# A planner that orders TensorE's work: due steps joined behind a generator's products, and new charges on its clock

## The chip, the core and the metric

The kernel runs on one core of a Trainium2 chip. Its engines are TensorE (PE: matmuls out of SBUF into PSUM), VectorE (DVE), ScalarE (ACT), GpSimd (POOL) and SyncE (SP, which issues DMAs). Each takes its instructions in the order in which the program emits them. The metric is device time of one execution, in microseconds (us); the median of three runs is given for the kernel before.

## What is computed

Two layers of a hybrid backbone over 256 context tokens and 256 latent tokens, width 2048, in float32. Cut to what matters here:

```python
for l in range(2):
    shift, scale, gate = split(silu(c) @ ada_w[l] + ada_b[l])        # for context and latent
    xn = rmsnorm(h) * (1 + scale) + shift
    u  = xn @ w_in[l]                      # one wide projection: r, k, v, pool, gates, decay, iclr, merge
    r, k, v = token-shifted parts of u
    S = S * w_t + (S @ -kk_t) (kk_t a_t)^T + v_t k_t^T               # a scan over the tokens,
    y = S @ r_t                                                      # 16 heads of 64, two directions
    y_a = (groupnorm(y) + bonus) * silu(gate_a) @ w_out_a
    y_b = (pool_mixer(u) * silu(gate_b)) @ w_out_b
    h = h + gate * ((mg0 * y_a + mg1 * y_b) @ w_out)
out = rmsnorm(h_lat) * final_g
```

In the second layer the context part is only needed up to its final state, so most products have 256 columns there instead of 512.

## The kernel before, in words

**Main stream.** The large projections are cut into units (class `Main`). A unit of 128 output channels runs over chunks of weights; each weight tile is loaded by SP (`wr`), rounded to `whi` by ACT, and DVE takes the rest as `wlo`. A step is three fp32r matmuls into `ps_mm` (`xh,whi`, `xl,whi`, `xh,wlo`). Loads are issued up to LA = 6 chunks ahead of the step that is emitted. `ps_st` is the group that starts a layer; `ps_ada` are the modulation's float32 products (128 rows by 2 or 4 columns), zipped into other units; `ps_mix` is the pool mixer.

**Generators.** The recurrence is done in chunks of 64 tokens for pairs of heads (8 pairs, each in two halves of four chunks). Python generators emit it step by step. `prep` makes the decays and keys of a pair (`ps_kk`, `ps_d`, `ps_a` of 512 columns, `ps_b`); `inv` inverts the chunk's triangular matrix by levels, in float16 (`ps_M`, then `ps_Z` and `ps_W` in turns, `ps_R`, `ps_X`, `ps_T`, `ps_V`); `chain` carries the state over the chunks (`ps_z`, `ps_a`, `ps_p`, `ps_y`, float32 products of 64 columns); `gnorm` is the group norm (`ps_c`, `ps_v`). Layer 1 runs two `inv` generators side by side, layer 0 one. Each step waits in the data for ACT or DVE work on the result of the step before it, and a generator yields the time at which its next step is due. For a step with products that is mostly `mg + rdy(inputs)`: the time at which the planner thinks the inputs are ready, plus a margin `mg` of 1000 ns in layer 0 and 600 ns in layer 1. A pair `(time, n)` also asks that n of the three PSUM buffers of the pool `piv` are free.

**The emission clock.** The order of everything is fixed while the program is built. `E["pe"]`, `E["dve"]`, `E["act"]` are clocks of the planner. Each emitted instruction moves its engine's clock (`clk`): to the latest of the engine's clock, the release of the output's buffer and the readiness of the inputs, plus a charge. A result is ready a lag later (200 ns behind PE, 140 ns behind ACT and DVE). None of this is executed on the chip; it only decides who comes next in each engine's queue.

**The loop `run`.** It goes through the generators in an order of priority (chain, gnorm, inverses, prep, open_y). The first whose due time is not later than `E["pe"]` is taken. If none is due, the main stream emits a batch of NS = 2 steps (six matmuls) if its weights are ready before the earliest due time; then the loop looks again. If the main stream isn't ready, the clock jumps to the earliest due time.

**The tiling of a matmul.** A matmul uses as many rows and columns of the array as its operands have: `128*128` in the rows of the trace is 128 rows by 128 columns. `ps_mm`, `ps_Z`, `ps_T` and the products of prep and gnorm are 128*128, `ps_W`, `ps_a` (64 columns) and one kind of `ps_y` 64*64, `ps_z`, `ps_p`, `ps_V` and the other `ps_y` 128*64, `ps_M` 64*128, `ps_ada` 128*4 or 128*2.

Of the kernel before, what the change touches and what calls it, by code (L numbers as in the profile page):

```python
# [8 lines left out]
R32 = mybir.dt.float32r  # L9
# [21 lines left out]
NU = (0, 1)  # L31
ZD = (0, 0)
N1, LA0, G0, LAG = 2, 20, 2, 4
AH, PACE, MG = 400.0, 600.0, (1000.0, 600.0)

V_MU, V_W0, V_A0, V_KK, V_KA, V_RK = 0, 24, 40, 56, 64, 80
# [10 lines left out]
def kernel(  # L47
# [65 lines left out]
    E = dict(pe=0.0, act=0.0, dve=0.0, pool=0.0, sp=0.0)  # L113
    rt, rd, old = {}, {}, {}

    def nm(ap):
        return ap.tensor.name
# [4 lines left out]
    def clk(eng, cost, o, ins, lag=60.0):  # L122
        t = max(E[eng], rd.get(old.get(nm(o)), 0.0))
        for a in ins:
            t = max(t, rt.get(nm(a), 0.0))
        t += cost
        E[eng] = t
        rt[nm(o)] = t + lag
        for a in ins:
            rd[nm(a)] = t + lag  # L130
# [29 lines left out]
    def size(ap):  # L160
        n = 1
        for s in ap.shape[1:]:
            n *= s
        return n

    def mm(out, lhsT, rhs, start=True, stop=True, dep=True):
        nc.tensor.matmul(out=out, lhsT=lhsT, rhs=rhs, start=start, stop=stop)  # L167
        n, m = size(rhs), size(lhsT)
        dt = lhsT.dtype
        if dt == F32:  # L170
            c = 110 if m <= 32 else 360 if n < 32 else 1.6 * n if n > 64 else 190 if m > 64 else 78
        elif dt == R32:
            c = max(0.4225 * n, 109) + 75 * (kind[0] != dt)
        else:
            c = 28 if m > 64 else 18
        kind[0] = dt
        clk("pe", c, out, (lhsT, rhs) if dep else (), 200.0)

    kind = [R32]

    def act(out, in_, func=AF.Copy, scale=1.0, bias=None):
        kw = {} if bias is None else dict(bias=bias)
        nc.scalar.activation(out=out, in_=in_, func=func, scale=scale, **kw)  # L183
        c = (50 if psum(in_) else 90) + 0.84 * size(out) + 93 * ((not isinstance(scale, float)) + (bias is not None))
        clk("act", c, out, (in_,), 140.0)
# [50 lines left out]
    def do_late(force=False):  # L236
        i = 0
        while i < len(late):
            if force or late[i][0] <= E["pe"]:
                late.pop(i)[1]()  # L240
            else:
                i += 1
# [247 lines left out]
    def proj(src, nk, rhs, ts_, post, ck=4, **kw):  # L490
        st = {}
        n = ts_.stop - ts_.start

        def pre():
            st["ps"] = pmm.tile([128, T], F32, tag="mm", name="ps_mm")

        def mk(k):
            def step(c):
                ps = st["ps"][:, 0:n]
                rh, rl = rhs(k)  # L500
                q = k % ck
                mm(ps, c["h"][:, q, :], rh[:, ts_], start=(k == 0), stop=False)
                mm(ps, c["h"][:, q, :], rl[:, ts_], start=False, stop=False)
                mm(ps, c["l"][:, q, :], rh[:, ts_], start=False, stop=(k == nk - 1))
            return (k // ck, step)

        return Unit(pieces(src, 2 * ck, ck), [mk(k) for k in range(nk)], pre, lambda: post(st["ps"][:, 0:n]), **kw)
# [4 lines left out]
    def due(x):  # L512

        return max(x[0], piv.free("iv", x[1])) if isinstance(x, tuple) else x

    def run():

        while True:
            do_late()
            best, bt, held = None, None, True  # L520
            for g in gens:
                while g[1] is None:
                    g[1] = next(g[0], "end")
                    if g[1] is None:
                        break
                    held = False
                if g[1] == "end" or g[1] is None:
                    continue
                t = due(g[1])
                if best is None or t < bt:  # L530
                    best, bt = g, t
                if t <= E["pe"]:
                    best, bt = g, t
                    break
            gens[:] = [g for g in gens if g[1] != "end"]
            if best is None or bt > E["pe"]:
                mt = M.time()
                if mt is not None and (best is None or max(mt, E["pe"]) <= bt):
                    for _ in range(NS):
                        M.step()  # L540
                        do_late()
                        mt = M.time()
                        if mt is None or mt > E["pe"] + SL:
                            break
                    continue
            if best is None:
                if not gens and M.empty():
                    break
                if late:
                    do_late(True)  # L550
                elif held:
                    raise RuntimeError("stuck")
                continue
            E["pe"] = max(E["pe"], bt)
            best[1] = next(best[0], "end")
        do_late(True)

# [91 lines left out]
    def phase_a(l):  # L649
# [7 lines left out]
        rhs = lambda k: (xh[k], xl[k])  # L657
# [5 lines left out]
        def chk(hf, j, d):  # L663
            return hf * 4 + (j if d == 0 else 3 - j)
# [300 lines left out]
        def inv(hfs, n16, nlo, zb):  # L965
            for p in range(NP):
                for hf in hfs:
                    while not fl["prep"][p]:
                        yield None
                    idx = p * 2 + hf  # L970
                    while fl["mm"] < idx or idx >= 2 and not fl["chain"].get((p - 1, hf)):
                        yield None
                    fl["mm"] = idx + 1
                    yield from inv_half(p, hf, n16, nlo, zb, hf if len(hfs) == 1 else 0)

        def inv_half(p, hf, n16, nlo, zb, u):
# [10 lines left out]
            for q in range(2):  # L987
                pm = [piv.tile([128, 2, 2, 128], F32, tag="iv", name="ps_M") for _ in range(2)]
                for j2 in range(2):
                    for d in range(2):  # L990
                        c = chk(hf, 2 * q + j2, d)
# [38 lines left out]
            ps = piv.tile([128, 8, 64], F32, tag="iv", name="ps_Z")  # L1030
# [17 lines left out]
            for lev in range(1, 6):  # L1048
                yield mg + rdy(X), 1
                ps = piv.tile([128, 8, 64], F32, tag="iv", name="ps_Z")  # L1050
# [30 lines left out]
            ps = piv.tile([128, 4, 2, 64], F32, tag="iv", name="ps_R")  # L1081
# [10 lines left out]
            ps = piv.tile([128, 4, 2, 64], F32, tag="iv", name="ps_X")  # L1092
# [15 lines left out]
            for q in range(2):  # L1108
                ps = piv.tile([128, 2, 2, 128], F32, tag="iv", name="ps_T")
                for j2 in range(2):  # L1110
                    for d in range(2):
                        c = chk(hf, 2 * q + j2, d)
                        nc.tensor.transpose(ps[:, j2, d, :], BK[:, d, c % 4].rearrange("p a t -> p (a t)"), ident)  # L1113
                        clk("pe", 120, ps, (), 200.0)
                act(BKt[:, 2 * q:2 * q + 2], ps)
            if last:
                yield from wait()
# [1 line left out]
            ps = pch.tile([128, 4, 64], F32, tag="ch", name="ps_V")  # L1119
# [381 lines left out]
    with tc.manual_schedule():  # L1501
# [68 lines left out]

        M.q2 += ada_blocks(1, KD, 2, pre0=to_1)
        run()
        B1 = A[2]
        rs = B1["p"].tile([128, TC], F32, tag="rs", name="rs")
# [112 lines left out]
```

## Time and profile before

| what | us |
|---|---|
| median of 3 runs (3052.47 to 3059.95) | 3058.64 |
| the profiled execution, its own time | 3058.09 |
| its span, first to last instruction | 3056.3 |
| busy: PE, PE's weight loads | 2906.3, 2292.5 |
| busy: DVE, ACT, POOL | 1820.7, 1457.3, 149.7 |
| mean granted TensorE clock, as a share of the full one | 0.978 |

A row of the timeline has the start in us from the span's start, a duration, engine and line, and what is written from what. Ends of matmuls are modelled, so neighbouring matmuls overlap in it and a difference of starts is the better measure of what one costs. A row of waits sums the idle time of an engine by the instruction that ended it.

### The profile page before, as it was taken

Reading aid. Unit: us, or ns where it says so; the run is one execution under the profiler, and the core shown is the slowest. Engines: PE = TensorE matmul, PEld = TensorE weight load, DVE = VectorE, ACT = ScalarE, POOL = GpSimd, SP = SyncE. Lnnn points to the kernel's source line nnn. Section 1 sums busy time; section 2 is a strip of 40 time slices with the busy share of each in tenths; the row PEclk is TensorE's granted clock in tenths of the full one; section 3 lists DMA queues with packets and bytes.
Section 4 is the critical chain, followed back from the end, with each engine's and each line's share of the span. In section 5 each row is a group of like instructions: output and inputs, shape, how many; then the busy total and the mean of one; then the engine's idle time right before and its main releaser. Section 6 shows DMA issues by size and latency. Waiting matters only on the chain.

```text
span 3056.3 us, 66262 instructions
## 1 busy us (share of the span) xinstructions
PE 2906.3 (95%) x27122; PEld 2292.5 (75%) x27122; DVE 1820.7 (60%) x4171; ACT 1457.3 (48%) x3092; POOL 149.7 (5%) x211
## 2 busy tenths in 40 slices
PE   5999999999999999998999989999999989999897
PEld 2687777767777777776876657887887768888797
DVE  3475666565655655534443235886786667775575
ACT  3254445445554554533222223666556646666454
POOL 2200000000000000000000002000000000000000
PEclk8999999999999999998999999999999989999899
DMA  9732222232333222327657764432333343344875
GB/s 361 256 121 72 78 76 91 72 116 94 112 111 118 87 80 87 94 88 248 205 190 225 234 222 124 141 117 85 108 94 111 119 127 99 111 122 129 260 251 161
DMA packets 158482, 427.74 MB, mean 140 GB/s; under 512 B 17376, under 2 KB 53600, under 8 KB 154080
## 3 DMA queue, kind: packets, MB, share of 16 engines
q1 hardware_dynamic: 133120, 390.32, 40.5%
q10 hardware_dynamic: 25056, 33.17, 3.0%
q8 instruction: 213, 3.49, 0.5%
q14 instruction: 93, 0.76, 0.1%
HBM read 389.21 MB, written 34.21 MB: 139 GB/s over the span
## 4 chain that ended last, share of the span: by engine, by line
PE 78%; DVE 8%; DMA 7%; ACT 5%; issue 2%; SPq 0%; POOL 0%; DVEq 0%; ACTq 0%; POOLq 0%
PE ps_mm L167 54%; PE ps_st L167 4%; DMA wr<-in_w_o 3%; DVE wlo L191 3%; PE ps_W L167 3%; PE ps_M L167 2%; PE ps_ada L167 2%; PE ps_y L167 2%; PE ps_a L167 2%; DMA wr<-in_w_in 2%; PE ps_Z L167 1%; PE ps_z L167 1%; PE ps_p L167 1%; ACT whi L183 1%; PE ps_T L1113 1%
## 5 line engine op out<-in xcount | busy, mean ns | idle before, releaser
L167 PE MATMUL ps_mm<-xh,whi 128*128 128x512 f32 (+1 forms) x2448 | 914.8, 374 | 8.2 <-ACT whi L183 3.1
L191 DVE TENSOR_TENSOR wlo<-wr,whi 128x512 fp32r<-128x512 f32 (+1 forms) x932 | 636.7, 696 | 444.8 <-ACT whi L183 439.1
L183 ACT ACTIVATE whi<-wr 128x512 fp32r<-128x512 f32 (+1 forms) x932 | 567.1, 619 | 671.3 <-PE ps_mm L167 336.7
L167 PE MATMUL ps_mm<-xh,wlo 128*128 128x512 f32 (+1 forms) x2448 | 855.2, 349 | 16.4 <-DVE wlo L191 15.7
L167 PE MATMUL ps_mm<-xl,whi 128*128 128x512 f32 (+1 forms) x2448 | 851.1, 348 | 0.0
L167 PEld LDWEIGHTS ps_mm<-xh,whi 128*128 128x128 f32 x2448 | 465.6, 190 | 91.9 <-issue 7.9
L167 PEld LDWEIGHTS ps_mm<-xh,wlo 128*128 128x128 f32 x2448 | 465.8, 190 | 83.5 <-DVE wlo L191 22.5
L167 PEld LDWEIGHTS ps_mm<-xl,whi 128*128 128x128 f32 x2448 | 467.6, 191 | 46.3 <-issue 1.0
L167 PE MATMUL ps_mm<-mgh,whi 128*128 128x512 f32 (+1 forms) x512 | 181.2, 354 | 2.9 <-ACT whi L183 2.9
L1024 DVE CAST_PREDICATED X<-pm_t,ps_W 128x128 f16<-128x128 uint8 x640 | 141.7, 288 | 65.2 <-PE ps_W L167 63.8
L167 PE MATMUL ps_mm<-mgh,wlo 128*128 128x512 f32 (+1 forms) x512 | 175.4, 343 | 0.0
L167 PE MATMUL ps_mm<-mgl,whi 128*128 128x512 f32 (+1 forms) x512 | 174.5, 341 | 0.0
L167 PE MATMUL ps_mm<-yh,whi 128*128 128x512 f32 (+1 forms) x512 | 129.0, 344 | 0.2 <-ACT whi L183 0.2
L167 PEld LDWEIGHTS ps_mm<-mgh,whi 128*128 128x128 f32 x512 | 98.2, 192 | 38.9 <-issue 19.3
L167 PE MATMUL ps_mm<-yl,whi 128*128 128x512 f32 (+1 forms) x512 | 125.4, 337 | 0.6 <-DVE m L195 0.5
L183 ACT ACTIVATE VS<-P 64x128 f32<-64x128 f32 x128 | 39.3, 307 | 167.3 <-DVE P L195 164.8
L183 ACT ACTIVATE zb<-ps_Z 128x512 f16<-128x512 f32 x144 | 85.2, 592 | 70.2 <-PE ps_Z L167 68.8
L167 PEld LDWEIGHTS <-X 64*64 64x64 f16 x2560 | 89.4, 110 | 35.7 <-issue 27.5
L191 POOL TENSOR_TENSOR nlo<-MM,n 64x512 f16<-64x512 f32 x48 | 62.8, 1308 | 1072.2 <-DVE X L1024 760.2
L167 PEld LDWEIGHTS ps_mm<-mgh,wlo 128*128 128x128 f32 x512 | 98.3, 192 | 14.5 <-DVE wlo L191 3.6
L167 PEld LDWEIGHTS ps_mm<-mgl,whi 128*128 128x128 f32 x512 | 98.4, 192 | 8.7
L167 PE MATMUL ps_ada<-wr,svp 128*4 128x256 f32 (+1 forms) x1024 | 83.2, 402 | 22.8 <-DMA wr<-in_ada_w 22.8
(258 smaller groups left out, 4353.2 us busy)
## 6 DMA issues: line engine op xcount, KB each, us to landing
wr<-in_w_in SPq DMA_DIRECT2D x306, 512.0 KB, 3.7
wr<-in_ada_w SPq DMA_DIRECT2D x128, 512.0 KB, 3.9
wbig<-in_ada_w SPq DMA_DIRECT2D x32, 1024.0 KB, 6.0
wr<-in_w_o SPq DMA_DIRECT2D x64, 512.0 KB, 4.8
wr<-in_w_b SPq DMA_DIRECT2D x32, 512.0 KB, 4.8
wr<-in_w_a SPq DMA_DIRECT2D x32, 512.0 KB, 4.0
wr<-in_w_st SPq DMA_DIRECT2D x32, 384.0 KB, 4.3
d_mg<-mth ACTq DMA_DIRECT2D x32, 256.0 KB, 2.0
```

Source lines behind the costliest of these rows:

```text
L167: nc.tensor.matmul(out=out, lhsT=lhsT, rhs=rhs, start=start, stop=stop)
L183: nc.scalar.activation(out=out, in_=in_, func=func, scale=scale, **kw)
L191: ENG[eng].tensor_tensor(out=out, in0=a, in1=b, op=op)
L1024: nc.vector.copy_predicated(dst.rearrange(pat, **kw)[:, :, :, u, :], m, src.rearrange(pat, **kw)[:, :, :, u, :])
L1113: nc.tensor.transpose(ps[:, j2, d, :], BK[:, d, c % 4].rearrange("p a t -> p (a t)"), ident)
```

## The change

`mm` gets new charges. It keeps the tiling of the product before (`mode`, each side rounded up to 32, 64 or 128) beside its type, charges 104 ns when the tiling changes, and 80 ns when an fp32r product follows another type at the same tiling. float32 products are charged by columns and by their share of the array. A transpose is charged 220 ns instead of 120. `count` counts the products. In `run`, `was` is the count at the end of the last main batch. While products of a generator have been emitted since (`count[0] != was`), steps that are due up to JOIN = 600 ns later than the clock are taken as well, by generators' priority; the clock is not moved forward to their due time. Behind a main batch the limit is the clock itself, as before.

```diff
+JOIN = 600.0
@@ mm
-        n, m = size(rhs), size(lhsT)
+        n, m, r = size(rhs), size(lhsT), lhsT.shape[0]
         dt = lhsT.dtype
+        up = lambda x: 32 if x <= 32 else 64 if x <= 64 else 128
+        mode = (up(r), 128 if dt == R32 else up(m))
         if dt == F32:
-            c = 110 if m <= 32 else 360 if n < 32 else 1.6 * n if n > 64 else 190 if m > 64 else 78
+            c = max(1.667 * n, 60) * mode[0] * mode[1] / 128 ** 2 * (2 if mode == (64, 64) else 1) + 5
         elif dt == R32:
-            c = max(0.4225 * n, 109) + 75 * (kind[0] != dt)
+            c = max(0.417 * n, 60) + 13
         else:
-            c = 28 if m > 64 else 18
-        kind[0] = dt
+            c = 29 if m > 64 else 16
+        c += 104 if mode != kind[1] else 80 if dt == R32 != kind[0] else 0
+        kind[:] = dt, mode
+        count[0] += 1
         clk("pe", c, out, (lhsT, rhs) if dep else (), 200.0)
-    kind = [R32]
+    kind = [R32, (128, 128)]
+    count = [0]
@@ run
+        was = -1
         while True:
             do_late()
+            now = E["pe"] + (JOIN if count[0] != was else 0)
...
-                if t <= E["pe"]:
+                if t <= now:
...
-            if best is None or bt > E["pe"]:
+            if best is None or bt > now:
...
+                    was = count[0]
                     continue
...
-            E["pe"] = max(E["pe"], bt)
+            E["pe"] = max(E["pe"], bt - JOIN if bt <= now else bt)
@@ inv_half
-                        clk("pe", 120, ps, (), 200.0)
+                        clk("pe", 220, ps, (), 200.0)
```

## Rows read from the trace of the kernel before

**Rows 1.** The head of the page and its first part: the span; busy time, share of the span and instructions of an engine.

```profile
span 3056.3 us, 66262 instructions
...
PE 2906.3 (95%) x27122; PEld 2292.5 (75%) x27122; DVE 1820.7 (60%) x4171; ACT 1457.3 (48%) x3092; POOL 149.7 (5%) x211
```

**Rows 2.** The page's fourth part: shares of the chain of work that ended last.

```profile
PE 78%; DVE 8%; DMA 7%; ACT 5%; issue 2%; SPq 0%; POOL 0%; DVEq 0%; ACTq 0%; POOLq 0%
```

**Rows 3.** The table by stage, for the two stretches in which generators run: start and end, length, busy us (instructions) of PE, PEld, DVE, ACT and POOL, granted clock, DMA share, GB/s.

```profile
190.00:1394.00 1204.00, 1187.39 (x11215) 892.72 (x11217) 695.83 (x1625) 577.83 (x1233) 43.99 (x55) 1.00 0.31 95
...
1900.00:2850.00 950.00, 900.22 (x10973) 766.10 (x10972) 688.25 (x1736) 577.40 (x1305) 48.33 (x58) 0.97 0.39 117
```

**Rows 4.** PE's timeline: the first product of the first and of the last visit of generators, of 335 in layer 0 and of 310 in layer 1.

```profile
203.01 0.38 PE L167 MATMUL ps_M<-AR,BK 64*128 64x128 f32 x2
...
1380.18 0.40 PE L167 MATMUL ps_v<-gqh,bo_r 128*128 128x512 f32 x1
...
1930.10 0.40 PE L167 MATMUL ps_kk<-kqh,bo_r 128*128 128x512 f32 x1
...
2835.03 0.58 PE L167 MATMUL ps_v<-gqh,bo_r 128*128 128x256 f32 x1
```

**Rows 5.** PE's timeline in layer 0: a main matmul, a visit of ps_W (first and last of its 16 rows), the first two main matmuls behind it.

```profile
599.77 0.39 PE L167 MATMUL ps_mm<-xh,wlo 128*128 128x512 f32 x1
600.09 0.22 PE L167 MATMUL ps_W<-zb,X 64*64 64x64 f16 x2
...
600.59 0.20 PE L167 MATMUL ps_W<-X,zb 64*64 64x64 f16 x2
600.71 0.50 PE L167 MATMUL ps_mm<-xh,whi 128*128 128x512 f32 x1
601.04 0.39 PE L167 MATMUL ps_mm<-xl,whi 128*128 128x512 f32 x1
```

**Rows 6.** PE's timeline in layer 0: a visit of ps_Z, one batch of the main stream (first two and last of its six matmuls), a visit of ps_z.

```profile
280.23 0.39 PE L167 MATMUL ps_mm<-xl,whi 128*128 128x512 f32 x1
280.46 0.39 PE L167 MATMUL ps_mm<-xh,wlo 128*128 128x512 f32 x1
280.69 0.41 PE L167 MATMUL ps_Z<-X,n 128*128 128x64 f16 x8
280.93 0.47 PE L167 MATMUL ps_mm<-xh,whi 128*128 128x512 f32 x1
281.24 0.39 PE L167 MATMUL ps_mm<-xl,whi 128*128 128x512 f32 x1
...
282.17 0.40 PE L167 MATMUL ps_mm<-xh,wlo 128*128 128x512 f32 x1
282.49 0.45 PE L167 MATMUL ps_z<-VS,MM 128*64 128x64 f32 x8
```

**Rows 7.** The same in layer 1, where the main matmuls have 256 columns: ps_Z, one batch, ps_a.

```profile
2597.69 0.28 PE L167 MATMUL ps_mm<-xh,wlo 128*128 128x256 f32 x1
2597.81 0.41 PE L167 MATMUL ps_Z<-X,n16b 128*128 128x64 f16 x8
2598.05 0.36 PE L167 MATMUL ps_mm<-xh,whi 128*128 128x256 f32 x1
2598.26 0.28 PE L167 MATMUL ps_mm<-xl,whi 128*128 128x256 f32 x1
2598.37 0.28 PE L167 MATMUL ps_mm<-xh,wlo 128*128 128x256 f32 x1
...
2598.73 0.28 PE L167 MATMUL ps_mm<-xh,wlo 128*128 128x256 f32 x1
2598.94 0.45 PE L167 MATMUL ps_a<-Zs,X 64*64 64x64 f32 x8
```

**Rows 8.** ACT's timeline: what wrote VS ahead of the ps_z of rows 6, and Zs ahead of the ps_a of rows 7; in brackets the idle time before it and who ended it.

```profile
279.86 0.31 ACT L183 ACTIVATE VS<-P 64x128 f32<-64x128 f32 x1 [1.22 <-DVE P L195]
...
2597.20 0.26 ACT L183 ACTIVATE Zs<-ps_z 128x128 f32<-128x128 f32 x1
```

**Rows 9.** PE's waits in 190 to 1394 us: who waited for whom, us in total, times, longest.

```profile
PE ps_ada L167 <- DMA wr<-in_ada_w: 8.0, 5, 3.3
PE ps_ada L167 <- DVE ada_r L206: 4.5, 6, 2.1
...
PE ps_p L167 <- DVE VS L200: 1.2, 2, 0.9
```

**Rows 10.** PE's timeline in layer 1: a visit with two steps, ps_W (its last row) and ps_p, and the main matmul behind it.

```profile
2600.72 0.20 PE L167 MATMUL ps_W<-X,zbb 64*64 64x64 f16 x2
2601.10 0.78 PE L167 MATMUL ps_p<-VS,BKt 128*64 128x64 f32 x8 [0.18 <-ACT VS L183]
2601.80 0.38 PE L167 MATMUL ps_mm<-xh,whi 128*128 128x256 f32 x1
```

**Rows 11.** PE's waits in 1900 to 2850 us: the main stream's longest, and the first and last of the twelve rows in which a generator's product waits (ps_T, ps_a, ps_b, ps_W, ps_z, ps_M, ps_Z, ps_p; 12.5 us together).

```profile
PE ps_mm L167 <- DVE wlo L191: 14.4, 15, 2.2
...
PE ps_T L1113 <- DVE MM L191: 3.0, 1, 3.0
...
PE ps_p L167 <- ACT VS L183: 0.2, 1, 0.2
```

## The prediction

> **What bounds the kernel.** I read the page first. PE is busy for 2906.3 of 3056.3 us, DVE for 1820.7 [rows 1], and 78% of the chain of work that ended last is PE [rows 2]. So a microsecond of PE time is a microsecond of the kernel, unless somebody else becomes late. The table by stage comes next: the generators (recurrence, inverses, preparation, group norm) run in two stretches, 190 to 1394 us (layer 0) and 1900 to 2850 us (layer 1), 2154 us together [rows 3]. Outside them there is nothing to join. The reader should note DVE: 695.8 of 1204 us (58%) in the first stretch, 688.3 of 950 us (72%) in the second.
>
> The PE timeline comes last, since it shows what a generator's visit costs. Call every run of generator products between two pieces of the main stream a visit. I walked along all the rows of PE and count 335 visits in layer 0 and 310 in layer 1; the first and last of each are in [rows 4]. Behind 106 of the 335 and 150 of the 310, the main stream put out one batch only (two steps, six or seven matmuls) before the next visit. Those are what the change can join.
>
> **The price of a visit.** Starts of neighbouring matmuls tell it. Main matmuls of 512 columns follow each other after 0.23 us, of 256 columns after 0.12. Into a visit whose tiling is not 128x128 the step is 0.32 (599.77 to 600.09), so 0.09 more. Out of it the last product takes 0.12 (600.59 to 600.71), where its pair took about 0.03 inside the visit (16 pairs from 600.09 to 600.59), so 0.09 to 0.10 more. The first main matmul behind it takes 0.33 (600.71 to 601.04), 0.10 more [rows 5]. Together 0.29 us. A visit of ps_Z keeps 128x128: it enters at 0.23 (280.46 to 280.69), but the first main matmul behind it takes 0.31 (280.93 to 281.24), so 0.08 to 0.09 [rows 6]; the same in layer 1, 0.21 for 0.12 (2598.05 to 2598.26) [rows 7]. A joined pair therefore saves 0.29 where both have one tiling, 0.19 where the tilings differ (one change stays between them), and 0.09 where one of the two is 128x128.
>
> A rule can be set against this. The rows show 0.31 behind ps_Z, with no tiling changed [rows 6]. The Trainium skill (TensorEngine Tiling (Array Packing), Key Properties) prices another thing: "Changing tiling mode (not just tile) drains the TensorE"; by it alone a joined ps_Z would save nothing. What that makes of the sum is a rival below; the sum itself goes by the rows.
>
> **Part 1, JOIN.** Behind products the planner also takes a step that is due within 600 ns. An example in layer 0: ps_z at 282.49 reads VS, which ACT finished at 280.17 (279.86 + 0.31) [rows 8]; with the lag of 0.14 and the margin of 1.0 in the code it was due at 281.31, that is 0.38 behind the end of the ps_Z visit at 280.93 [rows 6]. Joined, one return goes and ps_z still starts 0.76 us behind its input. In layer 1, ps_a at 2598.94 reads Zs of 2597.46; with 0.14 and 0.6 it was due at 2598.20, 0.15 behind 2598.05 [rows 7, 8].
>
> I did this for each visit behind a single batch whose input can be followed (lag left out). Layer 0: 45 of 89 would join, of which 34 have a 128x128 side, 7 differ, 4 are equal: 34 x 0.09 + 7 x 0.19 + 4 x 0.29 = 5.6 us, times 106/89 = 6.6. Layer 1: 80 of 131, 42, 14 and 24 of these kinds: 3.8 + 2.7 + 7.0 = 13.4 us, times 150/131 = 15.4. Another 11 visits behind two batches (3 and 8) give 2 us. Lower end: these 24 us. Upper end: a joined pair tends to stay joined, since both then wait for similar times; all 256 at the same means (0.12 and 0.17) give 13 + 25 = 38 us.
>
> In layer 0 nothing pays for it: the margin falls from 1.0 to 0.4 us at the least, and in the whole stretch only 1.2 us of PE's waits is for a generator's input [rows 9].
>
> In layer 1 the margin falls from 0.6 to nothing, and 51 of the 131 have inputs that came later than 0.6 would allow: run right behind the earlier visit, each would stall PE, 26.4 us in all, 0.5 each. The planner doesn't know this lateness. It charged 6 x 0.109 + 0.075 = 0.73 us for a batch of 256 columns, so its due times lie within 0.73 behind the visit; spread evenly, 600/730, some 107 of 131, join, 27 of them from the late ones. If they are the nearest 27, they stall about 5.5 us, if any 27, about 14; I take 9, times 150/131 = 10, and their joins save 27 x 0.17 x 1.15 = 5. A joint visit with such a stall is to be seen already: ps_p behind ps_W waits 0.18 at 2601.10 [rows 10].
>
> **Part 2, the clock's charges.** A 512-column main matmul is charged 226.5 ns instead of 216.3, a 256-column one 119.8 instead of 109.2 (the rows: 0.23, 0.12), and each change 104 ns where there were 75 once on the way back (the rows: 0.29 a visit). Nothing on the chip costs less by it; steps fall due after less main work. A visit and its batch in layer 1 last 0.89 us (2598.05 to 2598.94) [rows 7] and were charged 0.73, are charged 0.82 now (0.93 with the entry). Every step so loses 0.1 to 0.2 us of hidden slack. Layer 0 has plenty. In layer 1 PE's waits for generator inputs are 12.5 us now, in twelve rows [rows 11]; shifted by up to 0.2 us I price 5 more, between 0 (the next batch boundary often stays the same) and 12 (doubled). The main stream's own wait there is 14.4 us for DVE's wlo [rows 11]; denser generators at a DVE share of 72% make it 0 to 5 more; I take 0. The vector engines' charges aren't touched.
>
> The loads and stores that go along with moved steps cost nothing in the sum: in layer 0 PE waited for weights' DMAs only at ada (8.0 us in 5 waits) [rows 9], the main stream's loads are issued six chunks ahead, by position and not by this clock. If that cover went, the price is what ada pays now, 8 us a layer. Last, the end of the phases: generators end at 1380 and 2835 us [rows 4], before the output projections that need them, so a faster recurrence alone gives nothing.
>
> **The sum.** Layer 0: -6.6 and -0.7 for its share of the two-batch visits, -7. Layer 1: -15.4 - 1.3 - 5 + 10 + 5 = -7. Together -14 us. The profiled execution took 3058.1 us (span 3056.3 and 1.8 around it), by chance 0.5 below the median of 3058.6. Forecast: 3044 us.
>
> **Rivals.**
> *Stalls of layer 1 decide (slower).* Products that joined with no margin stand at the head of PE's in-order queue; behind them wait the main matmuls, and behind those ACT and DVE with the next whi and wlo. For it: the 51 late inputs, DVE's 72%. Against it: only 12.5 us of such waits today. With all 150 joined: 26.4 x 1.15 = 30 of stalls, 12 for slack, 5 for wlo, less the 25 saved and layer 0's 7: +15, 3073 us. It decides once a joined step in layer 1 stalls more than 0.22 us on the mean (the 0.17 saved and layer 0's 7 us over 150).
> *Only a change of tiling costs.* For it: the 0.09 in and 0.10 out [rows 5]. Against it: 0.31 behind ps_Z [rows 6]. Joins would save one or two changes of 0.10, and none with ps_Z: (7 + 8) x 0.1 x 1.19 + (14 + 48) x 0.1 x 1.15 = 9 us, less 15 of stalls and slack: +6, 3064. This is what the rule quoted above would give; the rows speak against it.
> *Little joins (no change).* The planner's due times aren't the trace's; once order shifts, steps may mostly come due over 600 ns behind a visit, as 95 of the 220 I could follow were. With a third of the joins and half the stalls: -8 + 8, 3058.
> *Joined pairs stay joined.* 38 us and only 10 of stalls: 3030.
>
> **How the numbers follow.** Forecast (3033 to 3049) 0.42; pairs stay joined (below 3033) 0.12; little joins 0.22; tiling alone 0.03; layer 1's stalls 0.21. A measurement tells about 0.3%, 9 us, from no change. Faster by more: 0.42 + 0.12 = 0.54; same: 0.25; slower: 0.21, as the stalls go beyond 3068 when they decide. The range for 8 in 10 goes from 3020 (all joins, no stalls) to 3072 (the slower rival's own time); the likeliest case's own is 3033 to 3049.
>
> **What would show it.** Visits: about 275 instead of 335 in layer 0, about 200 instead of 310 in layer 1, and hardly any main run of six matmuls between them. PE's waits for generator inputs stay near 1 us in layer 0 and rise from 12.5 to some 25 in layer 1. The stretch of layer 0 is 5 to 13 us shorter, that of layer 1 by 0 to 15. If layer 0 isn't shorter, the price of a visit or the count of joins is wrong; if layer 1 is longer with waits at ps_W, ps_Z, ps_a, the stalls decided; if wlo's 14.4 grew most, DVE did. Outside the two stretches nothing should move by more than 2 us; if it does, the new charges moved something that I held still.

## The result and the profile after

The changed kernel takes 3070.0 us (median of 5 runs, 3066.6 to 3077.6); the kernel before beside it 3054.2. The ratio is 1.0054, 95% interval 1.0041 to 1.0067: slower by about 16 us, where 14 us faster was forecast. The number lies inside the range given; the direction was wrong.

The profiled execution took 3066.6 us, the quickest of the five. The head of its page, beside [rows 1]:

```profile
span 3064.8 us, 66284 instructions
...
PE 2902.5 (95%) x27122; PEld 2297.3 (75%) x27122; DVE 1823.7 (60%) x4171; ACT 1457.4 (48%) x3092; POOL 152.4 (5%) x211
```

PE is busy 3.8 us less and the span is 8.5 us longer, so PE idles 162.4 us instead of 150.0. I split each span into three: PE's idle time; half of PE's busy time at the lower of its two clocks (1.2 of 2.4 GHz), which is about what that clock costs; and the rest, the work at full clock. Before: 150.0 + 45.8 + 2860.5. After: 162.4 + 51.7 + 2850.8. **The work did shrink, by 9.7 us. Waiting took back 12.4, the lower clock 5.9.** The three make +8.5, the difference of the two spans; the other 7 us or so of the medians' 16 aren't in these two traces, since the execution profiled before stood 4 us above its kernel's median and that after 3 us below. How far one such split can be trusted is seen in p1 below, where 99% of PE's steps stand in the order of the kernel before: its profiled execution is 8.7 us shorter than that of the kernel before, 4.5 of it idle time, 3.4 the lower clock and 0.8 work. So the work repeats to about 1 us, idle time and clock only to 3 to 5.

Joins came, but two in three of those forecast. PE's timeline in layer 0 after, a joint visit, two batches, the next joint visit:

```profile
281.93 0.39 PE L168 MATMUL ps_mm<-xh,wlo 128*128 128x512 f32 x1
282.25 0.45 PE L168 MATMUL ps_a<-Zs,X 64*64 64x64 f32 x8
282.63 0.41 PE L168 MATMUL ps_Z<-X,n 128*128 128x64 f16 x8
282.87 0.48 PE L168 MATMUL ps_mm<-xh,whi 128*128 128x512 f32 x1
283.19 0.39 PE L168 MATMUL ps_mm<-xl,whi 128*128 128x512 f32 x1
...
285.46 0.39 PE L168 MATMUL ps_mm<-xh,wlo 128*128 128x512 f32 x1
285.78 0.45 PE L168 MATMUL ps_y<-AR,P 64*64 64x64 f32 x8
286.16 0.45 PE L168 MATMUL ps_p<-VS,BKt 128*64 128x64 f32 x8
286.44 0.40 PE L168 MATMUL ps_y<-MM,VS 128*64 128x64 f32 x8
286.77 0.22 PE L168 MATMUL ps_W<-zb,X 64*64 64x64 f16 x2
```

The reader should see `chain` and `inv` side by side in each visit (ps_a with ps_Z, then ps_y, ps_p with ps_W), and one dear return, 282.87 to 283.19, where there were two as in [rows 6]. Visits fell from 335 to 291 in layer 0 and from 310 to 241 in layer 1, by 113 where the forecast had 170. Main runs of six matmuls, of which hardly any were to be left, went from 101 to 80 in layer 0 and from 146 to 44 in layer 1.

PE's waits after, in 190 to 1394 us, beside [rows 9]; the longest, and two of the six rows of generators:

```profile
PE ps_mm L168 <- ACT mth L189: 6.2, 4, 3.5
PE ps_ada L168 <- DVE ada_r L212: 5.3, 5, 1.7
...
PE ps_M L168 <- DVE MM L197: 1.3, 2, 0.7
PE ps_p L168 <- DVE VS L206: 1.1, 1, 1.1
```

And in 1900 to 2850 us, beside [rows 11]:

```profile
PE ps_mm L168 <- DVE wlo L197: 9.0, 16, 1.9
...
PE ps_mm L168 <- DVE gb L201: 5.3, 5, 2.2
PE ps_M L168 <- DVE X L1034: 5.2, 4, 1.4
...
PE ps_mm L168 <- ACT mth L189: 3.7, 3, 1.7
PE ps_z L168 <- DVE VS L212: 3.5, 4, 1.9
PE ps_p L168 <- ACT VS L189: 2.2, 2, 1.7
```

In layer 1 generators' products wait 21.0 us instead of 12.5; the forecast itself had some 25, the slower rival over 50. The main stream's waits fell there in all, from 21.2 to 19.5 us: those for wlo from 14.4 to 9.0, while those for ACT's and DVE's own work on its last result rose (gb from 2.5 to 5.3, mth from 1.3 to 3.7). In layer 0 the main stream's waits rose from 2.6 to 6.8 us, and 6.2 of these are for mth. The main stream's rows before, in layer 0 and then, beside the 14.4 for wlo of [rows 11], in layer 1:

```profile
PE ps_mm L167 <- DVE wlo L191: 1.3, 1, 1.3
PE ps_mm L167 <- ACT mth L183: 1.0, 2, 0.6
PE ps_mm L167 <- ACT whi L183: 0.3, 1, 0.3
...
PE ps_mm L167 <- ACT whi L183: 2.8, 3, 1.2
PE ps_mm L167 <- DVE gb L195: 2.5, 4, 0.8
PE ps_mm L167 <- ACT mth L183: 1.3, 2, 0.8
```

The longest wait for mth after, from the timeline of ACT and PE:

```profile
1032.47 0.40 PE L168 MATMUL ps_c<-yl,cm_r 128*128 128x512 f32 x1
...
1033.48 0.63 ACT L189 ACTIVATE whi<-wr 128x512 fp32r<-128x512 f32 x1 [3.10 <-DMA wr<-in_w_in]
1034.02 0.58 ACT L189 ACTIVATE yc<-ps_c 128x512 f32<-128x512 f32 x1
...
1035.83 1.44 ACT L189 ACTIVATE MM<-AR 64x256 f32<-64x256 f32 x4
1037.27 0.63 ACT L189 ACTIVATE whi<-wr 128x512 fp32r<-128x512 f32 x1
1037.81 0.58 ACT L189 ACTIVATE mth<-ps_mm 128x512 f32<-128x512 f32 x1
...
1038.44 0.50 PE L168 MATMUL ps_mm<-xh,whi 128*128 128x512 f32 x1 [3.52 <-ACT mth L189]
```

ACT stands 3.1 us at a weight tile that hasn't landed. Behind it, in one queue, are the group norm's yc and its squares, a generator's MM, the next whi, and last mth, which frees the PSUM buffer that PE needs. So two things stand ahead of mth, the late tile (3.1 us) and the work of the generators between the two whi (1034.02 to 1037.27, 3.25 us); which of them the 3.5 us are due to can't be told from this one place. Behind it the clock falls to its lower level (table by stage, columns as in [rows 3]):

```profile
1039.20:1046.00 6.80, 6.23 (x24) 4.69 (x24) 2.74 (x6) 2.25 (x4) 0.00 (x0) 0.50 0.34 116
```

There are 6.2 us of busy time at half clock behind this wait of 3.5 us. By the split above that is 3.1 us more, so the wait costs nearly as much again.

### The profile page after: what moved, and what is told of

Read it like the earlier page. It is cut to its first block, busy times and chain, and to the rows that moved or that the text cites. A ratio compares the mean times of both kernels' runs of the same rounds, so it can differ in the third digit from the quotient of the medians.

```text
span 3064.8 us, 66284 instructions
## 1 busy us (share of the span) xinstructions
PE 2902.5 (95%) x27122; PEld 2297.3 (75%) x27122; DVE 1823.7 (60%) x4171; ACT 1457.4 (48%) x3092; POOL 152.4 (5%) x211
## 5 line engine op out<-in xcount | busy, mean ns | idle before, releaser
L168 PEld LDWEIGHTS ps_mm<-xl,whi 128*128 128x128 f32 x2448 | 468.0, 191 | 47.6 <-issue 1.0
L168 PE MATMUL ps_mm<-mgl,whi 128*128 128x512 f32 (+1 forms) x512 | 173.3, 339 | 0.0
L189 ACT ACTIVATE VS<-P 64x128 f32<-64x128 f32 x128 | 39.4, 308 | 164.6 <-DVE P L201 163.5
L168 PEld LDWEIGHTS ps_mm<-mgh,wlo 128*128 128x128 f32 x512 | 97.6, 191 | 13.9 <-DVE wlo L197 3.3
```

## The experiments

All in one table. "No" and "all" under vector: ACT's and DVE's charges as they were, or times 1.15. Ratio to runs of the kernel before that were taken beside each, with its 95% interval; idle, half of the low-clock time and the rest as split above, from one profile each; visits that start in 190 to 1394 and in 1900 to 2850 us (where generators run on longer there are more behind that, up to 16 in f1). The rests that some expectations below name are by another count, with 2866 to 2869 for kernels without joins; only their differences can be held against the table.

| kernel | PE charges | vector | JOIN | margins | median us | ratio | idle | low clock / 2 | rest | visits |
|---|---|---|---|---|---|---|---|---|---|---|
| before | old | no | - | 1000, 600 | 3054.2 | 1 | 150.0 | 45.8 | 2860.5 | 335, 310 |
| p1 (main charge +0.5%) | old | no | - | 1000, 600 | 3055.0 | 1.0000 (0.9990 to 1.0011) | 145.5 | 42.4 | 2859.7 | 336, 311 |
| c1 (main charge +2%) | old | no | - | 1000, 600 | 3061.2 | 1.0026 (1.0015 to 1.0037) | 154.2 | 40.5 | 2862.4 | 332, 321 |
| c2 | old | no | - | 1040, 640 | 3029.1 | 0.9929 (0.9915 to 0.9943) | 135.1 | 34.8 | 2856.7 | 338, 317 |
| f3 | old | no | - | 1080, 680 | 3058.8 | 1.0015 (1.0006 to 1.0024) | 149.2 | 50.1 | 2861.4 | 336, 298 |
| e1 | old | no | 600 | 1000, 600 | 3042.3 | 0.9958 (0.9944 to 0.9971) | 152.3 | 36.3 | 2851.6 | 298, 244 |
| p2 | old | no | 560 | 1000, 600 | 3077.5 | 1.0076 (1.0064 to 1.0089) | 166.7 | 59.3 | 2852.2 | 300, 249 |
| c3 | old | no | 640 | 1000, 600 | 3066.1 | 1.0045 (1.0028 to 1.0063) | 168.1 | 59.5 | 2847.6 | 284, 236 |
| f4 | old | no | 600 | 1040, 640 | 3037.6 | 0.9945 (0.9933 to 0.9957) | 146.1 | 41.8 | 2847.9 | 295, 249 |
| e2 | new | no | 0 | 1000, 600 | 3063.0 | 1.0025 (1.0016 to 1.0034) | 157.0 | 41.9 | 2861.9 | 341, 317 |
| e3 | new | no | 600 in layer 0 | 1000, 600 | 3063.8 | 1.0034 (1.0021 to 1.0046) | 158.0 | 47.3 | 2856.8 | 292, 317 |
| e4 | new | no | 600 in layer 1 | 1000, 600 | 3066.5 | 1.0034 (1.0021 to 1.0046) | 161.6 | 41.5 | 2856.0 | 340, 241 |
| after | new | no | 600 | 1000, 600 | 3070.0 | 1.0054 (1.0041 to 1.0067) | 162.4 | 51.7 | 2850.8 | 291, 241 |
| c4 (main charge -2 ns) | new | no | 600 | 1000, 600 | 3066.1 | 1.0043 (1.0031 to 1.0056) | 164.6 | 49.1 | 2851.6 | 295, 242 |
| e6 | new | no | 600 | 1000, 900 | 3082.4 | 1.0091 (1.0078 to 1.0105) | 173.3 | 48.6 | 2857.3 | 292, 252 |
| f1 | new | no | 600 | 1600, 1200 | 3084.6 | 1.0098 (1.0084 to 1.0112) | 174.7 | 51.5 | 2848.9 | 305, 252 |
| f2 (products only) | new | no | 600 | 1000, 600 | 3080.6 | 1.0083 (1.0070 to 1.0096) | 175.4 | 48.6 | 2853.5 | 300, 254 |
| e5 | new | all | 600 | 1000, 600 | 3045.7 | 0.9970 (0.9960 to 0.9980) | 148.5 | 51.9 | 2846.1 | 308, 252 |
| g2 | new | all | 600 | 1040, 640 | 3042.7 | 0.9969 (0.9958 to 0.9980) | 147.4 | 47.1 | 2846.3 | 302, 256 |
| g1 | new | all | 0 | 1000, 600 | 3048.2 | 0.9986 (0.9976 to 0.9996) | 145.7 | 47.6 | 2853.2 | 334, 299 |

### The two parts and the two layers

Theory A said that joined products stall for want of margin, theory B that the new charges pull steps forward until ACT and DVE are late. e1 keeps the loop and puts the old charges back:

```diff
-            c = max(0.417 * n, 60) + 13
+            c = max(0.4225 * n, 109) + 75 * (kind[0] != dt)
...
-                    yield E["pe"] + 500
+                    yield E["pe"] + JOIN + 1
...
```

The last two lines are a step that only asks whether something is there yet. p2, c3, c4, e5, e6, f1, f4 and g2 have them too; e2, e3, e4, f2 and g1 have the 500 of the changed kernel.

> JOIN = 600 in the loop, all the old charges (a poll that yields E[pe] + 500 yields E[pe] + 601 instead, since a joined poll doesn't move the clock). Theory A, joined products stall for want of margin: most of the loss is here, 3062 to 3072 us, generator waits of layer 1 over 20 us. Theory B, the new charges pull steps forward until ACT and DVE are late for the main stream: this one is faster than before, 3038 to 3050 us, by the 0.12 to 0.17 us a saved visit.

e2 is the changed kernel with `JOIN = 0.0`.

> The new charges, JOIN = 0. Theory A: no change, 3050 to 3060 us, visits near 335 and 310. Theory B: the loss is here, 3064 to 3080 us, with the chain of layer 0 ending well before the 1370 us of before and PE waiting for ACT's and DVE's main work (mth, gb, whi, wlo) as in the changed kernel.

e3 and e4 join in one layer only:

```diff
-            now = E["pe"] + (JOIN if count[0] != was else 0)
+            now = E["pe"] + (join() if count[0] != was else 0)
+    def join():
+        return JOIN if not A[1] else 0.0      # e4: if A[1]
...
```

> The changed kernel with JOIN in layer 0 only. Theory A: layer 1's joins cost, so this is faster than the changed kernel by 8 to 16 us, 3050 to 3060 us. Theory B: it lies within 6 us of the changed kernel, or slower than it, since layer 1 loses its saved visits.

> The changed kernel with JOIN in layer 1 only. Theory A: as slow as the changed kernel plus layer 0's lost savings, 3072 to 3080 us. Theory B: charges alone, less layer 1's savings, 3060 to 3072 us.

Joins alone took 3042.3 us, 13 less than before, within 2 us of the forecast for the whole. Charges alone took 3063.0, nearly 8 more. If parts added up, the changed kernel would be 5 us faster than before; it is 16 slower. Theory A falls for e1. Theory B has e1 right and about half of the loss in e2. e3 (3063.8) and e4 (3066.5) miss what theory A gave them; e4 is where theory B put it, e3 6.2 us from the changed kernel where 6 were allowed. Neither theory has the 21 us between the sum of the parts and the whole.

### Whether one order says anything

e5 raises ACT's and DVE's charges beside PE's, e6 gives layer 1 more margin; p1 and p2 are small shifts as controls:

```diff
 def clk(eng, cost, o, ins, lag=60.0):
+        cost *= 1.15 if eng in ("act", "dve") else 1.0          # e5
...
-AH, PACE, MG = 400.0, 600.0, (1000.0, 600.0)
+AH, PACE, MG = 400.0, 600.0, (1000.0, 900.0)                    # e6
...
-            c = max(0.4225 * n, 109) + 75 * (kind[0] != dt)
+            c = max(0.4246 * n, 109) + 75 * (kind[0] != dt)     # p1, on the kernel before
...
-JOIN = 600.0
+JOIN = 560.0                                                    # p2, on e1
```

> The changed kernel with every charge of ACT and DVE times 1.15 (the traces have 619 to 627 ns for whi charged 520, 696 to 707 for wlo charged 603), polls at E[pe] + 601. Theory C, the new PE charges outran vector charges that were low by as much: with both raised the joins pay again, 3036 to 3050 us, generator waits in layer 1 back at 10 to 15 us. Theory D, the order is only reshuffled and each order has its own luck: anywhere from 3040 to 3075.

> The changed kernel with the margin of layer 1 at 900 instead of 600 ns, polls at E[pe] + 601. Theory C (lost slack): layer 1 gives back 10 to 20 us, 3045 to 3058 us, layer 0 as in the changed kernel (about 1235 us of main stream). Theory D: no order in it, 3040 to 3075, layer 0 moves too.

> Control: the kernel before, only the charge of a main matmul 0.5% higher (0.4246 for 0.4225 a column). Theory C: within 5 us of before, 3050 to 3060. Theory D: a shift of 5 to 15 us either way.

> Control: JOIN alone with the old charges, but 560 ns instead of 600. Theory C: within 5 us of JOIN alone, 3037 to 3047. Theory D: the gain of JOIN alone was partly luck, 3046 to 3058.

The vector charges that e5 raises are low by 17 and 21% in the two largest groups of DVE and ACT: the planner charges 603 ns for a wlo that takes 707, and 520 for a whi that takes 627 (groups of the kernel before; the mean ns stand behind the busy us):

```profile
L191 DVE TENSOR_TENSOR wlo<-wr,whi 128x512 fp32r<-128x512 f32 x868 | 602.6, 707 | 441.6 <-ACT whi L183 436.2 <-PE ps_R L167 0.5
...
L183 ACT ACTIVATE whi<-wr 128x512 fp32r<-128x512 f32 x868 | 535.3, 627 | 619.4 <-PE ps_mm L167 336.7 <-DMA wr<-in_w_o 163.8 <-DMA wr<-in_w_in 52.8
```

p2 is the warning: 40 ns less JOIN turned 13 us of gain into 22 of loss (3077.5). Its rest is that of e1 to 0.6 us; idle is 14.4 more and the clock 23. p1 gave 3055.0, but it is no test of luck: the charge has a floor of 109 ns, so that of a 256-column matmul didn't change (c1's 2% come to 1.2% there), and 99% of PE's steps stand in the order of the kernel before. e6 went to 3082.4, against theory C and above theory D's range as well; its layer 0 took as long as that of the changed kernel to 0.1 us (1235.1 of main stream in both), as theory C said. p1's layer 0, in nearly one order with that of the kernel before, was 3.2 us shorter, so an order repeats to a few us from run to run. e5's time, 3045.7, is as theory C had it. Its waits aren't: generators' waits in layer 1 were to go back to 10 to 15 us, and they are 24.5, more than the changed kernel's 21.0.

The next four ask how much any new order scatters, without joins (c1, c2) and with (c3, c4):

```diff
-            c = max(0.4225 * n, 109) + 75 * (kind[0] != dt)
+            c = max(0.4309 * n, 109) + 75 * (kind[0] != dt)     # c1, on the kernel before
...
-AH, PACE, MG = 400.0, 600.0, (1000.0, 600.0)
+AH, PACE, MG = 400.0, 600.0, (1040.0, 640.0)                    # c2, on the kernel before
...
-JOIN = 600.0
+JOIN = 640.0                                                    # c3, on e1
...
-            c = max(0.417 * n, 60) + 13
+            c = max(0.417 * n, 60) + 11                         # c4, on the changed kernel
```

> The kernel before with the charge of a main matmul 2% higher: no joins, old charges otherwise, a new order. Span less PE's waits and half its time at the lower clock was 2866 to 2869 us in the three kernels without joins, 2858 to 2859 in those with joins in both layers: 2866 to 2869 here too. Theory R, any new order has its own waits and the kernel before stands well among them: waits and clock up, 3060 to 3078 us. Theory W, only joins raise the waits: 3050 to 3060.

> The kernel before with both margins 40 ns longer (1040 and 640): no joins, a new order. As for the 2%: rest 2866 to 2869; Theory R 3060 to 3078 or well off 3055 on either side; Theory W 3050 to 3060, since more margin can only spare waits.

> JOIN alone at 640 ns, old charges. Rest 2856 to 2861. Theory R: anywhere in 3040 to 3078, between or beyond the 3042 of 600 ns and the 3077 of 560. Theory W: waits over 140 us, 3055 to 3078.

> The changed kernel with a main matmul charged 2 ns less (224.5 and 117.8), polls at E[pe] + 601. Rest 2856 to 2864. Theory R: off the changed kernel's 3070 by 5 to 25 us, either way. Theory W: within 6 us of it.

c2 ran in 3029.1 us, faster than both kernels by far, with no join in it. So orders scatter by some 30 us without joins, and theory R holds for c1 and c2. c3 (3066.1) fits both theories, and c4 (3066.1) is within 4 us of the changed kernel, as theory W had it; it also shows that the other poll and these 2 ns together change little. What scatters less is the rest: 2857 to 2862 (2860 in the mean) without joins under the old charges, 2846 to 2857 (2850 in the mean) in all kernels with joins in both layers, between them (2856 and 2857) with joins in one. The two ranges touch at c2 and e6. (g1, below, has 2853 without joins. There the recurrence's last product ends 105 us behind the last of layer 1's input projections, further than in any other kernel; in the kernel before it ends 1 us ahead of it. Whether that makes its rest smaller isn't shown.)

### What the extra waits come from

f1 gives joined products the old margin back, f2 joins only steps that emit products, f3 continues c2, f4 adds joins to c2:

```diff
-AH, PACE, MG = 400.0, 600.0, (1000.0, 600.0)
+AH, PACE, MG = 400.0, 600.0, (1600.0, 1200.0)                   # f1
...
-                if t <= now:
+                lim = now if isinstance(g[1], (tuple, Due)) else E["pe"]
+                if t <= lim:                                    # f2; mg + ... yields a Due
...
+AH, PACE, MG = 400.0, 600.0, (1080.0, 680.0)                    # f3, on the kernel before
...
+AH, PACE, MG = 400.0, 600.0, (1040.0, 640.0)                    # f4, on e1
```

> The changed kernel with margins 1600 and 1200, so that a joined product has the old margin at least (polls at E[pe] + 601). Lost margin is the cause: PE's waits for generator inputs in layer 1 fall from 21 to 10 to 14 us, all waits from 148 to 135 or less, 3040 to 3058 us. Vector work pulled forward is the cause: joined soft and paced steps still come 600 ns early, waits stay at 145 or more, 3060 to 3080 us. A slower chain may also end behind the fillers and hide in the gap at the end of a phase; then the stretch of layer 0 falls below 1228 us.

> The changed kernel, but only steps with a margin (those that emit products) are joined; steps of ACT and DVE alone fall due as before. Lost margin: like the changed kernel, waits 143 to 155 us, 3060 to 3075. Vector work pulled forward: waits below 140, 3045 to 3060. Visits 290 to 300 and 240 to 255 in both cases.

> The kernel before with margins 1080 and 680, no joins. If the gain of 40 ns more (3029) comes from the longer margin itself, 3020 to 3040 us; if that was one lucky order among many, 3045 to 3065.

> JOIN alone (old charges) with margins 1040 and 640, the best order so far plus joins. If what a join saves adds to a good order: 3015 to 3025 us, rest 9 us lower than without joins. If the order's scatter decides: 3030 to 3080, waits up from 120 to 140 or more.

f1 was the slowest of all, 3084.6 us. Its page and PE's waits in 1910 to 2840 us:

```profile
span 3075.1 us, 66214 instructions
...
PE 2900.4 (94%) x27122; PEld 2296.7 (75%) x27122; DVE 1823.8 (59%) x4171; ACT 1458.4 (47%) x3092; POOL 152.4 (5%) x211
```

```profile
PE ps_mm L168 <- DVE wlo L197: 18.1, 22, 2.1
PE ps_mm L168 <- ACT mth L189: 7.8, 4, 2.8
PE ps_mm L168 <- DVE gb L201: 4.8, 4, 1.8
PE ps_mm L168 <- ACT whi L189: 4.8, 6, 2.1
PE ps_T L1123 <- DVE X L1034: 2.7, 1, 2.7
```

The generators' waits in layer 1 did fall, from 21 to 14.5 us. The main stream's rose from 19.5 (21.2 in the kernel before) to 39: wlo, mth, gb and whi for the most part, work of DVE and ACT for itself. So f1 speaks against the lost margin as what made the change slower. f2 (3080.6) is slower than either account of it allowed, so it speaks against vector work that is pulled forward by itself; the vector work that comes with joined products stayed in. f3 (3058.8) shows c2 to have been one lucky order. f4 (3037.6) is fast again, rest 2847.9, but 8.6 us behind c2 and outside the 3015 to 3025 that it was given if savings add up.

The last two ask whether e5 was a cause or luck: g1 is e5 with `JOIN = 0.0`, g2 is e5 with margins 1040 and 640.

> The new PE charges with ACT's and DVE's raised by 15%, JOIN = 0. Theory C (PE's clock alone was raised): 3040 to 3057 us, less than the 3063 of the new PE charges alone; rest 2866 to 2869 as without joins, less what hides in the gap at a phase's end. Theory R (luck): 3055 to 3075.

> The changed kernel with ACT's and DVE's charges raised by 15% and margins 1040 and 640: another order of the same kind. Theory C: 3035 to 3057 us again, below all eight with PE's charges raised alone. Theory R: 3060 to 3085 as often as not.

Both times fell where theory C put them. e5's page, to be held beside that of f1, and the longest of its waits in 1910 to 2840 us:

```profile
span 3046.5 us, 66214 instructions
...
PE 2898.0 (95%) x27122; PEld 2293.3 (75%) x27122; DVE 1815.8 (60%) x4171; ACT 1454.5 (48%) x3092; POOL 155.1 (5%) x211
```

```profile
PE ps_mm L169 <- DVE wlo L198: 10.0, 15, 1.9
PE ps_z L169 <- DVE VS L213: 5.8, 5, 3.1
PE ps_ada L169 <- DVE ada_r L213: 5.0, 4, 2.5
```

PE's busy time is within 2.4 us of f1's, and idle is 148.5 us to 174.7. Against the changed kernel e5 idles 13.9 us less. Over the whole span its waits at ada are 48.2 us for 56.9, the main stream's 23.4 for 30.2, the generators' 25.8 for 24.5.

**What follows.** With PE's charges raised alone, all eight kernels were slower than before: 1.0025 without joins, 1.0034 with joins in one layer, 1.0043 to 1.0098 with joins in both. With ACT's and DVE's charges raised as well, all three were faster, by 0.14 to 0.31%: 0.9969 to 0.9986. Joins under the old charges went both ways (0.9945, 0.9958, 1.0045, 1.0076). So the slowness went with PE's charges raised alone, and most of it with the joins beside them.

The cause is not shown. I read it so: the planner's clocks were low by a like share before (in layer 1, 0.73 us charged for the 0.89 from 2598.05 to 2598.94 [rows 7]; 603 and 520 ns for wlo and whi that take 707 and 627), and raising PE's alone makes a vector result look ready after less main work than it needs; ACT's and DVE's queues then hold more ahead of the main stream's whi, wlo, mth. The main stream's waits fit this in layer 0 of the changed kernel (2.6 to 6.8 us), in f1 (39.1 in layer 1) and in e5 (5.6 and 15.4 in the two layers, where the changed kernel has 6.8 and 19.5). They don't in layer 1 of the changed kernel (21.2 to 19.5), and the generators' waits of e5, g1 and g2 (22.7 to 24.5 us in layer 1) are longer than the changed kernel's 21.0, where the reading has them shorter.

A rival stands beside it, the generators' pace. With PE's charges raised alone the recurrence of layer 1 ended 14 to 43 us ahead of the last input projection in seven kernels of the eight; with all charges raised it ended 50 to 105 us behind it, and behind it also in c2, e1 and f4 (10 to 32 us), the three fastest under the old charges. Three kernels speak against pace alone: f1 ended 62 us behind and is the slowest of all, f3 and p2 ended 47 and 8 us behind and weren't fast. ACT's and DVE's charges raised beside the old PE charges would part the two accounts; that wasn't run. Nor is it shown why e6, f1 and f2 came out 10 to 15 us slower still than the changed kernel. By the scatter of c1, c2, p2 and c3 that may be their orders' luck, and three kernels against eight are few.

## Why the prediction was wrong, point by point

**What bounds the kernel, and the price of a visit.** Right as far as they went. A return behind ps_Z still takes 0.32 us for 0.23, and the work at full clock fell in every kernel with joins. The Trainium skill (TensorEngine Tiling (Array Packing), Key Properties) says that a change of tiling drains TensorE, and gives no price. The 0.09 in and 0.10 out agree with it; that nothing else costs, which the rival made of it, doesn't agree with the 0.32.

**The size of the joins' saving (24 to 38 us).** This is the step that failed. The sum took 24 us and 5 more for the late inputs, 29 in all, and the work at full clock fell by 9.7. 291 and 241 visits came where 275 and 200 were forecast, 113 gone in all for 170, and each was worth 0.086 us (9.7 / 113), where the mean had been put at 0.12 and 0.17. Changes of tiling fell by only 53, from 1589 to 1536: most joined pairs had a 128x128 side or differed, and few were equal. By the price list, 113 returns at about 0.10 and 53 changes at 0.095 would be 16 us. All starts of PE at the full clock bear that out: what the steps into visits, out of them and behind them take beyond the usual step of the same product falls from 151 us to 126, and what changes of product inside visits take rises from 47 to 56, some 16 us net, or 0.14 a visit where the sum had 0.17. So the count was too high by half, the saving a visit by a fifth, and 6 of the 16 us don't show in the work. Where they went is open. A wait that is shorter than the modelled end of the matmul before it shows as no idle time, and may hide in the rest. With 16 in the place of 29 the prediction's own sum gives no change, with 9.7 it gives 5 us slower.

**"In layer 0 nothing pays for it."** Wrong. Generators' waits stayed small there (1.2 to 3.5 us), as forecast, but the main stream's rose from 2.6 to 6.8, and the stretch at the lower clock from 3.4 us to 10.2. The main stream of layer 0 took 1235.1 us instead of 1227.7, with charges alone 1235.0; 5 to 13 us less were forecast. I had looked only at who waits for a generator's input. A term that I put at nothing is the other way about: generators' work in ACT's and DVE's queues ahead of the main stream's own. The place at 1038.44 shows it, though beside a weight tile that came late to ACT, and the prediction had put the loads at nothing too.

**Layer 1's stalls (10 for joins, 5 for slack).** The mechanism is there, 12.5 to 21.0 us, 8.5 where 15 were put down. But f1 shows that paying it off with margin gained nothing.

**The charges (priced at 5 us of slack).** Alone they cost 7.7 us where 5 were put down, and the generators' waits in layer 1 rose by 6.2 (12.5 to 18.7), so by itself the term was near. What the sum doesn't have is what charges and joins do together, 21 us beyond the sum of e1 and e2: the four kernels with joins and the old charges have a mean ratio of 1.0006, the five with joins in both layers and PE's charges alone 1.0074. "The vector engines' charges aren't touched" stood there as a reason for calm; the three kernels with them raised are all faster than before. Which cause that has stays open. The 1.0006 also says that joins alone, in the mean of four orders, gained no time at all; the 13 us of e1 were a good draw. (Two figures of that paragraph are off and decide nothing: the floor makes the old charge of a 256-column matmul 109.0 ns, not 109.2, and a return behind ps_Z is charged 80 ns, not 104.)

**The lower clock.** Left out of the sum altogether. Half of PE's busy time at it went from 45.8 to 51.7 us here, and from 34.8 (c2) to 59.5 (c3) over the kernels. Behind the wait at 1038.44 it cost nearly as much as the wait.

**What made up the profiled 8.5 us.** 9.7 less work instead of 29; 12.4 more idle time and 5.9 more for the clock instead of 15 of stalls. The waits that the view of waits names grew by 13 us over the whole span: 10.8 before generators' products, 2.6 in the main stream and 2.3 at ada, with 2.4 less at ps_st. So the costs came out somewhat dearer than forecast, and in part in other places; the saving was a third of what it was put at.

**Outside the stretches, at most 2 us.** Between the input projections of the two layers 1.7 us less, behind the last of them 3.6 less, which is more than was allowed. What did it was not followed up.

**The rivals.** "Stalls of layer 1 decide" gave 3073 and 3070 came, but that is luck: it asked for 42 us of stalls and slack in layer 1, and 8.5 came. "Joined pairs stay joined" fell: 113 visits went, not all 256, and the gain it promised isn't there. "Little joins" fell too, with two thirds of the joins instead of one. "Tiling alone" gave 3064, but the 0.32 behind ps_Z speaks against it. A rival was missing: that a change of order alone moves this kernel by up to 23 us (c2), more than the whole effect that I added up.

## What to carry to other kernels

Where a planner fixes the order of in-order queues, a change to it is one draw from a scatter: find out how wide that is (here 3029 to 3061 us from shifts of 2% and 40 ns that mean nothing) before a gain of half a per cent is credited to a rule, and split the span into work, idle and clock, since the work part scattered least (3 to 14 us below the kernel before in the eleven kernels with joins in both layers, 10 in the mean; without joins c2 reached 4 and g1 7). Whether charges of a planner should be right relative to each other, rather than each as exact as it can be, is a thing to test: with one engine's made more exact while the others stayed low by 17 and 21%, all eight orders were slower, with all three raised all three were faster, and the cause wasn't separated. Before a saving is added up from pairs that could join, count how many will, since that count and the mix of pairs were what the sum had wrong. And a product brought forward costs not only its own wait: look at what its vector work stands in front of.

## What the runs showed of the hardware

Leaving a float16 ps_Z for an fp32r matmul costs 0.08 to 0.09 us though the tiling stays 128x128 (0.31 for 0.23, 0.21 for 0.12), almost as much as a change of tiling (0.09 to 0.10). And a wait can cost nearly twice: 6.2 us of busy time at half clock stood behind the wait of 3.5 us at 1038.44. Over the kernels PE's busy time at the lower clock ran from 70 us (c2, with 135 us of idle time) to 119 us (p2 and c3, with 167 and 168).
